# Reordering the token mixers of a two-layer hybrid backbone, with stated queueing

## The chip, the cores and the metric

One core of one Trainium2 chip runs the whole network in one launch. The metric is device time in microseconds (us). The engines are TensorE (PE: matmuls, and PEld: its weight loads), VectorE (DVE), ScalarE (ACT), GpSimd (POOL) and the DMA queue that SyncE (SP) issues. Each engine takes its instructions strictly in the order in which the program lists them.

## The reference, cut to what matters

Two layers; each is a half-step SwiGLU, a token mixer, and another half-step SwiGLU on 256 context and 256 latent tokens of width 1024. The mixer normalises, projects with one wide matrix `w_in`, runs four branches and merges them:

```
p = split(xn @ w_in)                       # ssm z, xbc, dt | mlstm qk, v, o, gates | s5 u | gdn qkv, z, b, a | 4 merge gates
ya = rmsnorm((ssd_scan(conv(xbc), dt) + d * x) * silu(z))          # ssm, chunks of 128, both directions
yb = rmsnorm(mlstm_scan(conv(qk), v, gates)) * sigmoid(o)          # ml
yc = glu(gelu(s5_scan(u)))                                         # s5: complex linear recurrence
yd = rmsnorm(gdn_scan(conv(qkv), beta, decay)) * silu(z)           # gdn: inverts a unit lower triangle per chunk
h += gate * ((sum_k sigmoid(g_k) * (y_k @ w_branch[k])) @ w_out)
```

Layer 0 needs all 512 tokens of the output; layer 1 needs only the 256 latent ones, so there many products have 256 columns instead of 512. All products are float32 in quality: each is three matmuls of values split into a high and a low part.

## The kernel before, in words

A projection (`proj`, L384) makes two output tiles of 128 rows. For it `weights` (L360) loads two blocks of weights by DMA on SP, ScalarE rounds each to its high part (L366), VectorE subtracts to get the low part (L371), and TensorE runs 48 matmuls (L380 to L382). Three buffers of weights run ahead. A projection that feeds a branch with a convolution ends in `conv`: four multiply-adds per tile on VectorE (L788). The normalised input lies in four tiles, the "x" slots (high and low, two each), with the context tokens in columns 0 to 255 and the latent ones in 256 to 511.

The branches are Python generators, and `mix` (L1749) runs them step by step by a string, `MIX_ORDER` (L1706): `ml:3` runs ml on by three yields, `i4` is the gdn projection of tiles 4 and 5, `g2` the eight tiles of merge gate 2, `m2` merges branch 2. The order in the string is a priority only. When the program is complete, a planner places every engine's instructions by a timeline of its own: whatever it believes ready goes first, and the string decides among what is ready. If it believes that an operation ends earlier than it does, an instruction that needs the result is placed early, and what stands behind it on that engine waits with it.

What the change touches:
- `gates` (L600), the step `rows`: per-token decays and gates; its transposes (L714) need an exponential on ScalarE (L711).
- `s5_scan` (L1593): 256 matmul records (L1606), 32 copies out of PSUM on ScalarE (L1614, L1615), then the recurrence, 63 times four operations of 128x64 on GpSimd (L1620 to L1623).
- `s5` (L1626): its first step copies the states on ScalarE (L1640, L1641) and VectorE (L1642 to L1644), then come four 1 MB tables, matmuls with them (L1661), and the gelu.
- `ml` (L965): uses GpSimd for a memset, for a copy and for weighting q (L1043); its matmuls are L1001, L1028, L1049 and L1054.
- `ssm` (L848): loads and transposes (L865), states, then one step per chunk (L904 to L936; matmuls L932), with products on VectorE (L925) and GpSimd (L927).
- `inverse` (L1085) in gdn: 31 steps of two operations on GpSimd (L1115, L1117), a DMA out (L1119) and back (L1125), and then matmuls.
- `merge_branch` (L1723): loads a branch's output into an x slot (L830), splits it into two more (L375, L376), and multiplies. An x slot is free only when the last projection that reads it is done.

Of the kernel before, what the change touches and what calls it, by code (L numbers as in the profile page):

```python
# [22 lines left out]
class Net:  # L23
# [227 lines left out]
    def rsqrt(self, y, src, scale):  # L251
# [108 lines left out]
    def weights(self, W, k0, nk, c0, nw=256):  # L360
# [17 lines left out]
    def mm3(self, out, ah, al, bh, bl, start, stop):  # L378
# [186 lines left out]
class Gates:  # L565
# [34 lines left out]
    def gates(self, l, P):  # L600
# [145 lines left out]
class Ssm:  # L746
# [100 lines left out]

    def ssm(self, l, P, G, o0, dz):  # L848
# [47 lines left out]
        y = self.t8(9, [128, 4, T])  # L896
        for c in range(o0, 4):
# [7 lines left out]
            for d in range(2):  # L905
                eg = self.t8(1 - d, [128, 2, 8, 128])
# [31 lines left out]
        z = self.get(2, dz, t0)  # L938
# [10 lines left out]
class Ml:  # L949
    def ml_in(self, l, P, o0):  # L950
        nc = self.nc
        W = self.A["w_in"][l]
        t0 = o0 * 128
        self.dM = self.scratch("mlqk", [4, 128, T])
        self.dV = self.scratch("mlv", [4, 128, T])
        self.conv_in(W, 1552, (2, 0), [t0, 0, 0, 0], P["ml_cw"], P["ml_cb"], self.dM)

        def done(c, p):
            v = self.kf([128, 256])
            nc.scalar.copy(v, p)  # L960
            nc.sync.dma_start(self.dV[c][:, j * 256:j * 256 + 256], v)
        for j in range(2):
            self.proj_tok(W, 2064 + j * 256, 8, done)

    def ml(self, l, P, G, o0, do):  # L965
# [9 lines left out]
        for c in range(4):  # L975
            nc.gpsimd.memset(va[c][:, :, 128:130], 1.0)
# [12 lines left out]
        for e in range(2):  # L989
            nc.gpsimd.tensor_copy(so[e * 64:e * 64 + 64], sov[e * 64:e * 64 + 64, :, :, :, e])  # L990
# [24 lines left out]
        for c in range(o0, 4):  # L1015
# [15 lines left out]
            for d in range(2):  # L1031
# [38 lines left out]
        self.rsqrt(ss[:, o0:], ss[:, o0:], 1.0 / 128)  # L1070
# [13 lines left out]
class Gdn:  # L1084
    def inverse(self, LT):  # L1085
# [840 lines left out]
```

## Time and profile before

| | us |
|---|---|
| median of 3 runs (2892.4 to 2896.47) | 2895.95 |
| the profiled execution | 2895.82 |
| its span, first to last instruction | 2894.1 |

| engine | busy us | share |
|---|---|---|
| PE | 2727.4 | 94% |
| DVE | 1664.8 | 58% |
| ACT | 1134.2 | 39% |
| POOL | 781.0 | 27% |

The mean granted TensorE clock is 0.965 of full speed. The mixer of layer 0 takes about 480 to 1245 us of the span, that of layer 1 about 2108 to 2695; the SwiGLU parts lie around them. In a table by stretches a row gives the stretch, its length, busy microseconds of each engine with the number of its instructions in brackets, the granted clock (1.00 is 2.4 GHz, 0.50 is 1.2 GHz), the busy share of the DMA engines and GB/s. A row of waits gives the waiting instruction, what released it, the sum, the number of waits, and the longest.

### The profile page before, as it was taken

To read this page: it belongs to the slowest core of one execution; us is meant where nothing else is said; L and a number is where in the kernel's file an instruction comes from. 1 tells how busy PE (TensorE), PEld (TensorE's weight loads), DVE (VectorE), ACT (ScalarE), POOL (GpSimd) and SP (SyncE) were. 2 spreads that over 40 slices of the span, in tenths; PEclk is the share of its full clock that TensorE was granted. 3 is DMA by queue.
4 is the path that set the end of the run, shared out by engine and by line. 5 is a ranking of instruction groups with operands and counts; after the bars stand their busy time and mean duration, and the time that the engine had idled before them with its cause. 6 is when DMAs were issued, how large, how long until landed. Compare 5 with 4: busy or idle time off the path is not lost.

```text
span 2894.1 us, 46233 instructions
## 1 busy us (share of the span) xinstructions
PE 2727.4 (94%) x17710; PEld 2287.2 (79%) x17710; DVE 1664.8 (58%) x3035; ACT 1134.2 (39%) x1743; POOL 781.0 (27%) x1210
## 2 busy tenths in 40 slices
PE   7999999979998999999999999999988789979999
PEld 5777679767776878796768897778977678978999
DVE  6655345456975546574333476554553788756655
ACT  4322224634544533242212353223455456633444
POOL 1442001492002361430000014420107812634100
PEclk9999999998999999999999999999999899989999
DMA  8444878545545554557763353453484467754554
GB/s 264 122 155 138 271 264 225 136 127 175 175 149 157 157 149 138 194 178 260 239 225 95 99 164 120 133 157 96 155 196 131 133 200 212 225 161 149 172 186 146
DMA packets 509820, 494.19 MB, mean 171 GB/s; under 512 B 79380, under 2 KB 437838, under 8 KB 508574
## 3 DMA queue, kind: packets, MB, share of 16 engines
q1 hardware_dynamic: 509598, 491.22, 56.2%
q8 instruction: 140, 2.29, 0.3%
q14 instruction: 82, 0.67, 0.1%
HBM read 429.17 MB, written 61.96 MB: 170 GB/s over the span
## 4 chain that ended last, share of the span: by engine, by line
PE 69%; POOL 12%; DMA 6%; issue 5%; DVE 4%; ACT 3%; SPq 1%; POOLq 0%; DVEq 0%; ACTq 0%
PE ffn.pb L380 15%; PE ffn.pb L381 15%; PE ffn.pb L382 15%; PE ffn.ps L187 2%; POOL s5scan.t L1623 2%; POOL s5scan.s5m L1620 2%; POOL s5scan.s5m L1622 2%; POOL s5scan.s5m L1621 2%; POOL gdn.t L1117 2%; POOL gdn.gpr L1115 2%; DMA ssm.t<-rows.rowd 1%; PE gates.pb L380 1%; PE gates.pb L381 1%; PE gates.pb L382 1%; PE merge.pb L380 1%
## 5 line engine op out<-in xcount | busy, mean ns | idle before, releaser
L371 DVE TENSOR_TENSOR ffn.wl<-ffn.wf,ffn.wh 128x1024 fp32r<-128x1024 f32 (+1 forms) x308 | 370.3, 1202 | 376.2 <-ACT ffn.wh L366 368.6
L366 ACT CAST ffn.wh<-ffn.wf 128x1024 fp32r<-128x1024 f32 (+1 forms) x308 | 310.4, 1008 | 554.1 <-PE ffn.pb L382 398.8
L382 PE MATMUL ffn.pb<-ffn.t,ffn.wh 128*128 128x256 f32 (+1 forms) x1312 | 438.4, 336 | 0.0
L381 PE MATMUL ffn.pb<-ffn.t,ffn.wl 128*128 128x256 f32 (+1 forms) x1312 | 438.1, 336 | 0.0
L380 PE MATMUL ffn.pb<-ffn.t,ffn.wh 128*128 128x256 f32 (+1 forms) x1312 | 434.5, 337 | 1.0 <-ACT ffn.t L344 1.0
L380 PEld LDWEIGHTS ffn.pb<-ffn.t,ffn.wh 128*128 128x128 f32 x1312 | 244.0, 189 | 34.4 <-ACT ffn.wh L366 4.2
L382 PEld LDWEIGHTS ffn.pb<-ffn.t,ffn.wh 128*128 128x128 f32 x1312 | 246.4, 188 | 29.9 <-issue 2.4
L381 PEld LDWEIGHTS ffn.pb<-ffn.t,ffn.wl 128*128 128x128 f32 x1312 | 247.2, 188 | 28.3 <-issue 1.6
L380 PE MATMUL ffn.pb<-wout.t,ffn.wh 128*128 128x256 f32 (+1 forms) x720 | 242.5, 338 | 0.9 <-ACT wout.t L344 0.9
L381 PE MATMUL ffn.pb<-wout.t,ffn.wl 128*128 128x256 f32 (+1 forms) x720 | 241.3, 336 | 0.0
L382 PE MATMUL ffn.pb<-wout.t,ffn.wh 128*128 128x256 f32 (+1 forms) x720 | 238.9, 335 | 0.0
L313 POOL TENSOR_TENSOR norm.kf<-norm.kf,norm.kf 128x256 f32<-128x256 f32 x45 | 41.9, 930 | 517.9 <-ACT norm.kf L311 506.8
L381 PE MATMUL gates.pb<-ffn.t,gates.wl 128*128 128x512 f32 (+1 forms) x512 | 174.6, 342 | 3.4 <-DVE gates.wl L371 3.4
L380 PE MATMUL gates.pb<-ffn.t,gates.wh 128*128 128x512 f32 (+1 forms) x512 | 173.7, 342 | 0.3 <-ACT gates.wh L366 0.3
L382 PE MATMUL gates.pb<-ffn.t,gates.wh 128*128 128x512 f32 (+1 forms) x512 | 173.9, 341 | 0.0
L380 PEld LDWEIGHTS ffn.pb<-wout.t,ffn.wh 128*128 128x128 f32 x720 | 137.4, 191 | 26.5 <-ACT ffn.wh L366 7.5
L381 PEld LDWEIGHTS ffn.pb<-wout.t,ffn.wl 128*128 128x128 f32 x720 | 136.1, 189 | 16.2 <-DVE ffn.kf L497 0.8
L382 PEld LDWEIGHTS ffn.pb<-wout.t,ffn.wh 128*128 128x128 f32 x720 | 135.0, 188 | 16.0 <-issue 0.8
L380 PE MATMUL ffn.pb<-t,ffn.wh 128*128 128x512 f32 x352 | 142.1, 404 | 2.0 <-DVE ffn.kf L492 1.9
L381 PE MATMUL ffn.pb<-t,ffn.wl 128*128 128x512 f32 x352 | 142.4, 405 | 0.0
L382 PE MATMUL ffn.pb<-t,ffn.wh 128*128 128x512 f32 x352 | 139.5, 402 | 0.0
L371 DVE TENSOR_TENSOR gates.wl<-gates.wf,gates.wh 128x1024 fp32r<-128x1024 f32 x64 | 82.8, 1296 | 61.5 <-ACT gates.wh L366 61.1
(573 smaller groups left out, 6332.9 us busy)
## 6 DMA issues: line engine op xcount, KB each, us to landing
ffn.wf<-in_ffn_up_dram SPq DMA_DIRECT2D x176, 512.0 KB
ffn.t<-in_ada_w_dram SPq DMA_DIRECT2D x68, 1024.0 KB
ffn.wf<-in_ffn_down_dram SPq DMA_DIRECT2D x104, 512.0 KB
gates.wf<-in_w_in_dram SPq DMA_DIRECT2D x64, 512.0 KB
merge.wf<-in_w_branch_dram SPq DMA_DIRECT2D x32, 512.0 KB
zs.wf<-in_w_in_dram SPq DMA_DIRECT2D x24, 512.0 KB
gdnin.wf<-in_w_in_dram SPq DMA_DIRECT2D x24, 512.0 KB
wout.wf<-in_w_out_dram SPq DMA_DIRECT2D x24, 512.0 KB
```

Of the source, the lines that this page charges most:

```text
L187: nc.tensor.matmul(pm[32 * k:32 * k + 32, :], lhsT=self.sF[:, h * 4 + k, 28 - 4 * i:60 - 4 * i], rhs=ws[h][:, k], start=(h == 0), stop=(h ...
L366: nc.scalar.copy(wh[:, :nk, :nw], wf[:, :nk, :nw])
L371: self.w_split = nc.vector.tensor_tensor(wl[:, :nk, :nw], wf[:, :nk, :nw], wh[:, :nk, :nw].bitcast(F32), op=OP.subtract)
L380: mm(out, lhsT=ah, rhs=bh, start=start, stop=False)
L381: mm(out, lhsT=al, rhs=bh, start=False, stop=False)
L382: mm(out, lhsT=ah, rhs=bl, start=False, stop=stop)
L1115: pt_(pr, Lo[:, j + 1:, j].unsqueeze(2).to_broadcast([128, n, m]), Z[:, j, :m].unsqueeze(1).to_broadcast([128, n, m]), op=OP.mult)
L1117: pt_(Z[:, j + 1:, :m], Z[:, j + 1:, :m], pr, op=OP.subtract)
L1620: tt(m[:, 0], at(n - 1), P["A8"][:, 0], op=OP.mult)
L1621: tt(m[:, 1], at(n - 1)[:, ::-1], P["A8"][:, 1], op=OP.mult)
L1622: tt(m[:, 0], at(n), m[:, 0], op=OP.add)
L1623: tt(at(n), m[:, 0], m[:, 1], op=OP.add)
```

## The change

1. The order is written in finer units (two tiles: `q0`, `v0`, `c2`, `zS0`, `ga1` to `gd1` for a quarter of a merge gate), and a step can be marked. `'` puts its TensorE instructions behind the last matmul of the projection traced before it; `!` puts also its ScalarE, VectorE and SP instructions behind that projection's rounding, subtraction and weight load. There are 16 marked steps in layer 0 and 12 in layer 1.
2. ssm runs before the s5 outputs: s5's three steps follow ssm's last one, the first marked `!`. ssm writes its output over its input and uses other slots; the s5 tables get four slots instead of two.
3. `rows` and the inverse are cut into more steps, so that their matmuls can be placed later.
4. ml uses no GpSimd: memset, copy, the product L1043 and the small power (L258) go to VectorE.
5. Half of the 32 copies of `s5_scan` (L1615) go from ScalarE to VectorE.
6. The inverse is split by columns: the first 12 on VectorE, the others on GpSimd.
7. In layer 1 the merges use halves of the x tiles: branch output and splits of the first two lie in the context columns, which no projection reads after the convolutions.

```diff
+        self.w_cast = nc.scalar.copy(wh[:, :nk, :nw], wf[:, :nk, :nw])
...
+        self.last_mm = mm(out, lhsT=ah, rhs=bl, start=False, stop=stop)
...
-        self.rsqrt(ss[:, o0:], ss[:, o0:], 1.0 / 128)
+        self.rsqrt(ss[:, o0:], ss[:, o0:], 1.0 / 128, 0)
...
-            pr = self.gp.tile([128, 256], F32, tag="gpr", name=self.nm("gpr"), bufs=2)[:, :n * m].rearrange("p (a b) -> p a b", a=n)
-            pt_(pr, Lo[:, j + 1:, j].unsqueeze(2).to_broadcast([128, n, m]),
+            for op, c0, c1 in ((nc.vector.tensor_tensor, 0, min(j + 1, 12)), (pt_, 12, j + 1)):
+                m = c1 - c0
...
-                    nc.scalar.copy(o(slice(64, 128), slice(31, None, -1)), pv[64:128, :, :, cs])
+                    nc.vector.tensor_copy(o(slice(64, 128), slice(31, None, -1)), pv[64:128, :, :, cs])
...
-            tb = self.t8(1 + b % 2, [128, R, m, 256])
+            tb = self.t8((5, 6, 1, 2)[b], [128, R, m, 256])
...
-    "rows load s5in s5scan oM loc mlin ml:3 s5:1 ml:1 ssmin s5:1 ml:3 zS i4 glu ssm:2 i6 ssm:3 i8 ssm:1 "
-    "i10 gdn:1 i2 i0 ssm:1 gdn:2 g1 gdn:11 g2 g0 zG out g3 m1 m2 m3 m0",
-    "load rows s5in s5scan mlin loc oM ml:4 ssmin s5:1 ml:1 s5:1 ml:2 i4 i6 zS ssm:2 glu ssm:2 gdn:1 "
-    "ssm:3 i8 i10 i0 i2 gdn:12 zG gdn:1 g1 g2 g0 g3 out m2 m1 m3 m0",
+    "rows:1 load s5in oM0 s5scan rows:1 oM2 loc q2 q0 v0 v1 ml:2 c0 'ml:1 c2 'ml:1 c4 'ml:1 c6 'ml:1 zS0 zS2 'ml:1 i4 "
+    "'ssm:1 i6 'ssm:1 i8 'ssm:1 i10 'ssm:1 i2 'ssm:1 i0 'ssm:1 ga1 'ssm:1 !s5:1 gb1 's5:1 gc1 s5:1 gdn:1 gd1 gdn:1 ga2 "
+    "gdn:6 glu gb2 gc2 gd2 ga0 gb0 gc0 gd0 zG0 zG2 ga3 !gdn:1 gb3 'gdn:6 gc3 gd3 out m1 m2 m3 m0",
+    "load rows:1 s5in q2 s5scan q0 'rows:1 v0 loc v1 oM0 oM2 ml:2 c0 'ml:1 c2 'ml:1 c4 c6 ml:1 zS0 'ssm:1 zS2 i4 'ssm:1 "
+    "i6 'ssm:1 i8 'ssm:1 i10 'ssm:1 !s5:1 i0 i2 's5:1 zG0 s5:1 zG2 gdn:1 ga2 gdn:1 gb2 gdn:6 "
+    "gc2 glu gd2 ga1 gb1 gc1 gd1 ga0 gb0 gc0 gd0 !gdn:1 ga3 gb3 'gdn:6 gc3 gd3 out m2 m1 m3 m0",
...
+HALVES = ((0, 1, 2), (3, 0, 1), (2, 4, 5), (3, 6, 7))
...
+            yH, yL = (self.half(i, F32R) for i in HALVES[S["n"]][1:])
...
+    def half(self, i, dt):
+
+        c = i // 4 * 256
+        t = (self.xH + self.xL)[i % 4][:, :, c:c + 256]
...
+            f, behind = f.lstrip("'!"), {"'": 1, "!": 4}.get(f[0], 0)
+            with ExitStack() as st:
+                for h in (self.last_mm, self.w_cast, self.w_split, self.w_dma)[:behind]:
+                    st.enter_context(self.tc.issue_after(h.ins))
+                step(f)
```

## Rows read from the trace of the kernel before

**Rows 1.** Busy time by stretches: layer 0 in three, layer 1 in three.

```profile
480.00:550.00 70.00, 63.98 (x558) 53.57 (x557) 25.75 (x68) 44.33 (x74) 6.79 (x30) 0.91 0.83 174
550.00:850.00 300.00, 274.75 (x1487) 225.25 (x1486) 213.05 (x439) 131.01 (x203) 117.97 (x256) 0.94 0.51 155
850.00:1245.00 395.00, 370.10 (x2295) 306.56 (x2294) 214.42 (x361) 148.65 (x233) 151.20 (x149) 0.96 0.52 156
2108.00:2200.00 92.00, 80.42 (x769) 72.80 (x768) 43.13 (x98) 56.83 (x94) 19.53 (x51) 0.93 0.70 161
2200.00:2440.00 240.00, 196.87 (x1367) 169.14 (x1366) 179.66 (x357) 115.50 (x196) 126.56 (x246) 0.90 0.56 164
2440.00:2695.00 255.00, 224.04 (x2107) 218.82 (x2107) 166.94 (x297) 114.91 (x191) 119.22 (x133) 0.91 0.65 189
```

**Rows 2.** What TensorE waited for, whole span; the longest nine sums within the mixers.

```profile
PE merge.pb L380 <- ACT merge.t L375: 15.1, 1, 15.1
PE ml.ps L1054 <- POOL ml.k L1043: 14.7, 4, 6.2
PE ssm.ps L932 <- DVE ssm.t L925: 13.8, 8, 6.1
PE ml.ps L1049 <- DVE ml.t L1037: 12.2, 1, 12.2
PE ssm.ps L865 <- DMA ssm.t<-ssmin.ssm: 8.5, 3, 6.8
PE ml.ps L1001 <- POOL s5scan.s5m L1622: 8.0, 1, 8.0
PE rows.ps L714 <- ACT rows.k L711: 6.7, 1, 6.7
PE s5scan.ps L1606 <- ACT s5scan.t L1615: 6.6, 6, 2.0
PE s5.ps L1661 <- ACT s5.t L1641: 6.1, 2, 5.0
```

**Rows 3.** What VectorE, ScalarE and the DMA queue waited for on GpSimd.

```profile
DVE s5.t L1642 <- POOL s5scan.t L1623: 15.2, 1, 15.2
...
DVE s5.t L1642 <- POOL s5scan.t L1623: 13.1, 1, 13.1
...
ACT s5.t L1640 <- POOL s5scan.t L1623: 15.3, 1, 15.3
...
SPq L1119 <- POOL gdn.t L1117: 13.3, 1, 13.3
```

**Rows 4.** Groups by line, ScalarE, 526 to 552 us: count, busy us, mean ns.

```profile
L1614 ACT COPY s5scan.t<-s5scan.ps 64x256 f32<-64x256 f32 x16 | 9.6, 600 | 0.3
L1615 ACT COPY s5scan.t<-s5scan.ps 64x256 f32<-64x256 f32 x16 | 9.5, 592 | 0.2
```

**Rows 5.** Three stretches of 10 us, columns as in rows 1.

```profile
590.00:600.00 10.00, 10.00 (x70) 9.16 (x69) 0.00 (x0) 0.29 (x1) 8.82 (x30) 1.00 0.08 29
640.00:650.00 10.00, 6.54 (x33) 5.26 (x31) 7.69 (x15) 4.87 (x9) 9.37 (x17) 1.00 0.25 79
...
2530.00:2540.00 10.00, 10.00 (x91) 10.00 (x90) 7.41 (x8) 5.61 (x8) 9.37 (x9) 1.00 0.84 252
```

**Rows 6.** GpSimd, layer 1: the recurrence's first operation (start, us), and the inverse by lines.

```profile
2184.87 0.33 POOL L1620 TENSOR_TENSOR s5scan.s5m<-s5scan.t,prep.a 128x64 f32<-128x64 f32 x1 [18.30 <-ACT s5scan.t L1615]
...
L1117 POOL TENSOR_TENSOR gdn.t<-gdn.t,gdn.gpr 128x31 f32<-128x31 f32 (+15 forms) x31 | 24.6, 793 | 2.4
...
L1115 POOL TENSOR_TENSOR gdn.gpr<-gdn.t 128x31 f32<-128x31 f32 (+15 forms) x31 | 22.7, 732 | 24.1 <-DMA gdn.t<-gdn.gl 21.8
```

**Rows 7.** Groups by line, VectorE: two products of two tensors, long and short.

```profile
L1008 DVE TENSOR_TENSOR ml.t<-ml.t,ml.mso 128x260 f32<-128x260 f32 x4 | 1.9, 486 | 3.9 <-ACT ml.t L1006 3.9
...
L268 DVE TENSOR_TENSOR gdn.rsq<-gdn.rstd 128x16 f32<-128x16 f32 x3 | 0.5, 174 | 0.1
```

More of the change, by code (lines that the diff above doesn't have):

```diff
@@ L1759, in mix @@
         order = MIX_ORDER[l].split()
-        last = [f for f in order if f == "out" or f[:4] == "ssm:" or f == "ssm"][-1].split(":")[0]
+        last = [f for f in order if f == "out" or "ssm:" in f][-1].lstrip("'!").split(":")[0]
         merged = lambda j: S["merged"][0][:, j] if l else S["merged"][j // 4][:, j % 4]
         self.dG = self.scratch("gdn", [12, 128, T])
+        self.dS = self.scratch("ssm", [8, 128, T])
+        self.dM = self.scratch("mlqk", [4, 128, T])
+        self.dV = self.scratch("mlv", [4, 128, T])
+        S.update({n: self.scratch(n, [4, 128, T]) for n in ("oM", "zS", "zG")})
         self.dGt = {}
-        make = {"ml": lambda: self.ml(l, P, S["G"], o0, S["oM"]), "s5": lambda: self.s5(l, P, S["G"], o0),
-                "ssm": lambda: self.ssm(l, P, S["G"], o0, S["zS"]), "gdn": lambda: self.gdn(l, P, S["G"], o0)}
+        make = {"rows": lambda: self.gates(l, P),
+                "ml": lambda: self.ml(l, P, self.G, o0, S["oM"]), "s5": lambda: self.s5(l, P, self.G, o0),
+                "ssm": lambda: self.ssm(l, P, self.G, o0, S["zS"]), "gdn": lambda: self.gdn(l, P, self.G, o0)}
+        zs = {"oM": (2576, self.sig_in), "zS": (0, self.silu_in), "zG": (5152, self.silu_in)}
         def step(f):
@@ L1805, in step @@
                 y = {0: self.dssm, 1: self.dml, 2: self.ds5, 3: S["y3"]}[k]
+                S["n"] = S.get("n", -1) + 1
                 if k < 3 or last == "ssm":
[L1807 removed]
+                    if l:
+                        src, y = y, self.half(HALVES[S["n"]][0], F32)
+                        for j in range(4):
+                            nc.sync.dma_start(y[:, j], src[j][:, t0:])
+                    else:
+                        y = self.get("x", y, t0)
                 if "merged" not in S:
                     S["merged"] = [self.t8(9, [128, 8, 256])] if l else [self.t8(8), self.t8(9)]
[L1810 removed]
+                self.merge_branch(l, P, k, y, merged, o0, not S["first"], S)
                 S["first"] = True
@@ L1813, in step @@
                 raise ValueError(f)
+        stages = {"load": "s5scan", "glu": "s5", "loc": "s5", "out": "gdn"}
+        kinds = {"g": "gates", "i": "gdnin", "m": "merge", "c": "ssmin", "q": "mlin", "v": "mlin", "o": "zs", "z": "zs"}
         for f in order:
+            f, behind = f.lstrip("'!"), {"'": 1, "!": 4}.get(f[0], 0)
             n = f.split(":")[0]
-            self.stage = {"load": "s5scan", "glu": "s5", "loc": "s5", "out": "gdn", "oM": "zs", "zS": "zs", "zG": "zs"}.get(
-                n, {"g": "gates", "i": "gdnin", "m": "merge"}[f[0]] if f[0] in "gim" and f[1].isdigit() else n)
-            step(f)
+            self.stage = n if n in make or n in ("s5in", "s5scan") else stages.get(n) or kinds[n[0]]
+            with ExitStack() as st:
+                for h in (self.last_mm, self.w_cast, self.w_split, self.w_dma)[:behind]:
+                    st.enter_context(self.tc.issue_after(h.ins))
+                step(f)
         self.stage = "wout"
```

119 lines of the change are left out of this document (60 added, 59 removed).

## The prediction, made before the changed kernel was run

> **What bounds the kernel now.** I read the engines' shares first: TensorE is busy 94% of the span, so a change of order can only win TensorE's idle time and its slow time. Then the busy time by stretches [rows 1]: outside the two mixers TensorE is almost always busy, inside them it is not. In layer 0 the idle time is 70.0 - 63.98 = 6.0, 25.3 and 24.9 us, in layer 1 11.6, 43.1 and 31.0: 142 us in all. After idle time the rows show a granted clock below 1.00. What that costs is at most (1 - clock) times TensorE's busy time: 5.8 + 16.5 + 14.8 + 5.6 + 19.7 + 20.2 = 83 us, less where the slow time fell into idle time. So 142 + 83 = 225 us is the most that this change could ever bring.
>
> Then the waits of TensorE [rows 2]. The nine listed make 15.1 + 14.7 + 13.8 + 12.2 + 8.5 + 8.0 + 6.7 + 6.6 + 6.1 = 91.7 us of the 142; the remaining 50 us are many small ones. Three of the nine name GpSimd or its recurrence only indirectly, so I asked who waits for GpSimd [rows 3]. VectorE stood 15.2 us in layer 0 and 13.1 in layer 1 at the state copies of s5 (L1642), ScalarE 15.3 us at L1640, and SP 13.3 us at the DMA out of the inverse (L1119). That is the pattern of the whole kernel: an instruction that needs GpSimd's result stands too early in an in-order queue, and what TensorE needs (ml's products at L1037, weight splits, the load for the first merge) stands behind it. The planner thinks GpSimd faster than it is.
>
> **The change, part by part.**
>
> 1. *s5's first step goes behind ssm, and ml leaves GpSimd.* With L1640 and L1642 behind ssm's last step, the recurrence should have ended when they come. ml's product L1043 no longer queues behind it. From rows 2 go 14.7 (L1054), 12.2 (L1049) and 8.0 (L1001): 34.9 us, all of it. VectorE gets these small operations, a few us in each layer; in the same rows its load is 180 of 240 us at the highest [rows 1], and I price this under 7. The reciprocal root of 8 elements in layer 1 becomes twelve VectorE operations of about 0.17 us [rows 7], 2 us beside projections: nothing.
>
> 2. *`rows` cut in two.* In layer 1 the transposes L714 stood in TensorE's queue ahead of mlin's matmuls and waited 6.7 us for an exponential. Now they are stated behind `q0`. All 6.7 go.
>
> 3. *Half of the copies to VectorE.* 16 x 0.600 + 16 x 0.592 = 19.1 us of ScalarE [rows 4] become 9.6, beside 16 copies on VectorE, which has 25.75 us of work in the 70 us of layer 0's first stretch and 43.13 of 92 in layer 1's [rows 1]. The 6.6 us at L1606 shrink with ScalarE's part, which is still as long as the matmuls between: I take 5. Nothing would go if a strided copy on VectorE took 1.2 us, twice ScalarE's 0.600; all 6.6 if it took less than that 0.600.
>
> 4. *ssm ahead of the s5 outputs.* The 6.1 us at L1661 (ScalarE's copies after the recurrence) go. But at the new place the copies, then two of the four table loads, have only one projection as cover, and two of the tables need slots that ssm gives back last. The trace shows no such place. From below it costs nothing (the copies move under `gb1`); from above what L1661 waits now, 6.1, in each layer. I take 4 per layer, 8.
>
> 5. *Marked ssm steps.* TensorE waits 13.8 us at L932 in 8 waits and 8.5 us at L865 (loads that wait for a slot or for the convolution's DMA). With a whole projection queued ahead of each chunk, VectorE and GpSimd get that projection's time to make the operands. In layer 1 the load has only `zS0`, 256 columns. I take half of 22.3, so 11. Full gain is the other end; the other is zero, if VectorE is late anyway.
>
> 6. *Inverse by columns, and merges in halves.* In layer 1 the inverse's POOL operations take 24.6 + 22.7 = 47.3 us [rows 6]. Step j has (31 - j)(j + 1) products, 5456 in all; columns from 12 on are 1330 of them in 19 steps. So GpSimd keeps 38 of 62 operations and 24% of the elements: between 0.24 x 47.3 = 11.4 us and 38/62 x 47.3 = 29. VectorE gets 62 operations with 4126/31 = 133 elements on average. Nearest rows: 0.174 us for 16 elements, 0.486 for 260 [rows 7]; linearly 0.32 us, 62 x 0.32 = 20 us (10.8 to 30). Even with GpSimd and VectorE in turn this is no longer than now. Before, TensorE had run out of projections; now `gc2` to `gd0` stand between, ten units and glu, eleven times 48 matmuls at 91 per 10 us [rows 5], 58 us. SP's 13.3 us at L1119 end while weights are still there, and the first two merges of layer 1 no longer need the x slots that the last gate reads. The 15.1 us at L380 go, all. If that cover were gone (inverse in turn and 20 us late) 15 would come back.
>
> 7. *What is paid.* VectorE: from 2200 to 2440 us it has 179.7 us of work [rows 1]. Its own work hardly moves out of there, and ml's products come in. If this stretch gave back its share of everything it would shrink to some 200 us, VectorE at 90%. Convolutions and ssm or ml chunks now alternate strictly, so I take back 20 us over both layers. Each of the 28 marked steps can also make TensorE stand at a chunk that VectorE has not finished. Seven are ml's; today's mean wait at an ssm chunk, 13.8 / 8 = 1.7 us [rows 2], gives 7 x 1.7 = 12. The gdn scan at the end keeps its small waits but may lose some merge matmuls as filler: 8, an estimate, about the sum of two waits of 4.
>
> Sum of idle time: 34.9 + 6.7 + 5 + 6.1 + 11 + 15.1 = 78.8, and a third of the unlisted 50, 17: 96 us, 68% of 142. Clock: 68% of 83 is 56; a slow stretch partly lies in the idle time already counted, so three quarters, 42. Gross 138. Back: 8 (under 4) + 20 + 12 + 8 = 48. Net 90. Against the profiled execution's own 2895.82 us this is 2805.8; the median of the runs, 2895.95, is the same within 0.13. I forecast 2806 us.
>
> A rule that speaks against the change: GpSimd and VectorE do not simply work side by side. With VectorE idle the recurrence makes 30 operations in 10 us, with VectorE busy 7.69 of 10 only 17 [rows 5]. The Trainium skill ("SBUF — State Buffer", section on the two separate sides) says why: VectorE with two SBUF inputs and GpSimd reading SBUF exclude each other for a whole instruction. The rows agree with a loss of that kind. By the rule the split inverse takes the sum of its parts, 31 us or more, not the longer part, 20; both are under the cover. What it could change is the recurrence, the second rival.
>
> **The rivals.**
>
> *All gaps close.* VectorE keeps up and the marked steps cost nothing: 96 + 56 and a little more of the small waits, 150 us, 2746. For it: in 850 to 1245 us and at the end VectorE is at 54% and 65% only [rows 1]. Against: 2200 to 2440.
>
> *VectorE becomes the bound and holds GpSimd back.* The copies that made VectorE stand 13 to 15 us [rows 3] are gone, so it works more while the recurrence runs. It has 4 x 63 = 252 operations. At 17 per 10 us all of it takes 148 us, at 30 it takes 84. In layer 1 it starts at 2184.87 now [rows 6], after 2 and 3 (6.7, and half of 19.1) about 16 us earlier, 2169, and ends at 2253 to 2317. ssm's first chunk wants its products L927 behind it on GpSimd. Between lie `q0` to `i6`: seven units of full width and six of half, 7 x 10.6 + 6 x 5.3 = 106 us, and ml's and ssm's own matmuls; so from 2275 on. Late by up to 40 us, 1 is not won but moved to ssm: 12.2 us and half of 14.7, 19.6, stay in layer 1, 5's 11 too, and 15 of the clock; 46 less than forecast: 2852.
>
> *Slower.* The place: TensorE's queue at the 28 marked steps. Projections behind a marked step wait for it, as they need not now, and a mark is worth nothing where VectorE comes later than the projection ahead ends. Without any wait at marked steps the change wins 138 - 8 - 20 - 8 = 102 us. Each us of mean wait costs 28, and slow clock in today's proportion (1 + 83/142 = 1.58), 44 us. So it decides at 102 / 44 = 2.3 us for each step. At the 3.7 us that L1054 waits on average now (14.7 / 4, rows 2) it costs 163: 61 us slower, 2957. For it: L932's longest wait, 6.1. Against: its mean, 1.7 [rows 2], and my 11 + 12 us over the 19 steps of ml and ssm is 1.2.
>
> *It doesn't do what it says.* The planner keeps its wrong idea of GpSimd and finds another early place for the marked steps' successors; or the halves of x are held as whole tiles. Then the idle time only changes its place: 2896.
>
> **How the numbers follow.** The forecast (2770 to 2838) has 0.53, all gaps close (2700 to 2770) 0.13, VectorE bound (2838 to 2872) 0.20, smaller gains (2872 to 2890) 0.02, no change 0.04, slower 0.08. Three runs of this kernel span 0.14%, so about 0.2% (5.8 us) is what a measurement tells from no change. Faster is 0.53 + 0.13 + 0.20 + 0.02 = 0.88. The range reaches from the middle of the first rival past the end of the second, 2730 to 2880.
>
> **What would show it.** Right: no wait of VectorE or ScalarE on the recurrence above 3 us; no wait of ml's matmuls on GpSimd; the first merge of layer 1 begins while gates still run; the clock in both mixers at 0.95 or more; ScalarE with 16 copies in s5_scan. Wrong: waits of TensorE on VectorE at L932, L1049 or the new place of L1661 with sums above 30 us; ssm waiting for GpSimd; VectorE above 90% between layer 1's second convolution and its gates with TensorE below 80%. The prediction fails as a whole if the mixers' idle time stays above 110 us.

## The result, and the profile after

The changed kernel takes 2850.91 us (median of 4 runs, 2845.56 to 2852.84) against 2894.76 of the kernel before beside it: ratio 0.985, 95% interval 0.983 to 0.986. That is 44 us faster, half of the 90 that were forecast. The time lies in the range, but outside the forecast's own range of 2770 to 2838. The profiled execution takes 2849.91 us, its span 2848.2.

The busy time by stretches, the same six as in [rows 1], with ends moved to where these parts now lie (columns as there):

```profile
477.00:549.00 72.00, 66.18 (x589) 55.85 (x590) 36.48 (x94) 32.83 (x57) 14.32 (x47) 1.00 0.74 166
549.00:800.00 251.00, 234.39 (x1250) 192.73 (x1249) 190.91 (x397) 110.97 (x182) 109.47 (x217) 0.97 0.52 156
800.00:1217.00 417.00, 397.69 (x2506) 329.83 (x2505) 259.21 (x478) 169.63 (x258) 129.31 (x129) 0.95 0.54 167
2079.00:2160.00 81.00, 71.52 (x708) 64.58 (x707) 49.43 (x116) 37.56 (x64) 15.97 (x46) 0.94 0.68 161
2160.00:2390.00 230.00, 205.13 (x1459) 179.58 (x1458) 189.19 (x376) 122.61 (x204) 125.08 (x236) 0.95 0.62 188
2390.00:2649.00 259.00, 221.66 (x2078) 217.08 (x2078) 179.01 (x363) 115.80 (x197) 96.94 (x109) 0.90 0.60 179
```

TensorE's idle time (length minus PE) is now 5.8 + 16.6 + 19.3 in layer 0 and 9.5 + 24.9 + 37.3 in layer 1: 113 us, 29 less than the 142 before. The clock's cost, worked out as in the prediction, falls from 83 to 7 + 20 + 4 + 10 + 22 = 63 us. Together this is 49, about the 44. The last stretch of layer 1 got worse: 37.3 us idle, 31.0 before.

The waits of TensorE within the mixers, nine longest sums and two small ones, against [rows 2]:

```profile
PE gdn.ps L1150 <- DMA gdn.k<-gdn.gz: 16.8, 1, 16.8
PE ssm.ps L930 <- DVE ssm.t L923: 8.9, 9, 1.8
PE s5scan.ps L1606 <- DMA s5scan.t<-prep.s5K: 8.1, 1, 8.1
PE ml.ps L1042 <- issue: 7.3, 2, 6.9
PE zs.pb L380 <- ACT zs.wh L366: 6.3, 2, 5.3
PE zs.pb L381 <- DVE zs.wl L371: 5.8, 4, 2.9
PE gates.pb L381 <- DVE gates.wl L371: 5.7, 2, 4.0
PE mlin.pb L380 <- ACT mlin.wh L366: 5.2, 1, 5.2
PE merge.pb L380 <- DVE merge.t L1754: 4.6, 3, 2.7
...
PE s5scan.ps L1606 <- DMA s5scan.t<-s5in.s5U: 2.4, 1, 2.4
...
PE ssm.ps L863 <- DMA ssm.t<-ffn.ssm: 2.0, 2, 1.4
```

("issue" is time in which the engine waited for nothing that the profile shows.) ml's waits on GpSimd are gone, so are those of `rows` and of s5's outputs. The wait for the inverse (L1150, the products behind the DMA out of it and back) has grown from 4.7 us to 16.8. New are the loads of the s5 scan (L1606) and most of the waits for weights that are rounded (L366) or split (L371): 6.3 + 5.8 + 5.7 + 5.2 + 1.3 = 24.3 us, 7.1 before. No wait of VectorE or ScalarE on the recurrence [rows 3] is left.

The inverse in layer 1, its products and its subtractions (start of the first and of the last, and median time of one), against [rows 6]:

```profile
L1114 DVE TENSOR_TENSOR gdn.gpr<-gdn.t x31: 170/335/561, 2478.1 to 2530.2; 128x60 f32<-128x60 f32 x2, 128x156 f32<-128x156 f32 x2, 128x192 f32<-128x192 f32 x2, 128x31 f32<-128x31 f32 x1
L1114 POOL TENSOR_TENSOR gdn.gpr<-gdn.t x19: 221/370/1320, 2478.2 to 2501.9; 128x19 f32<-128x19 f32 x2, 128x36 f32<-128x36 f32 x2, 128x51 f32<-128x51 f32 x2, 128x64 f32<-128x64 f32 x2
...
L1116 DVE TENSOR_TENSOR gdn.t<-gdn.t,gdn.gpr x31: 170/340/822, 2479.4 to 2530.4; 128x60 f32<-128x60 f32 x2, 128x156 f32<-128x156 f32 x2, 128x192 f32<-128x192 f32 x2, 128x31 f32<-128x31 f32 x1
```

VectorE's 62 operations take 21.0 us in sum but stand over 52 us, because other work of VectorE's lies between them in its queue, 15 weight subtractions of 19.7 us above all. GpSimd's part ends at 2502. TensorE has no projection left at 2518.6 and stands until 2535.4. Its clock falls during this stand; stretches of the changed kernel around it, and three of VectorE's busiest:

```profile
2200.00:2250.00 50.00, 47.06 (x295) 40.23 (x292) 45.42 (x102) 23.94 (x36) 46.63 (x86) 0.97 0.46 127
2250.00:2300.00 50.00, 45.86 (x231) 37.02 (x229) 48.25 (x96) 23.70 (x42) 29.00 (x44) 1.00 0.64 197
2300.00:2350.00 50.00, 45.96 (x369) 41.77 (x367) 46.59 (x89) 28.06 (x50) 3.90 (x3) 0.97 0.61 189
...
2478.00:2531.00 53.00, 36.12 (x303) 35.01 (x301) 49.34 (x107) 18.23 (x24) 30.91 (x46) 0.92 0.79 248
...
2519.00:2523.00 4.00, 0.00 (x0) 0.00 (x0) 4.00 (x8) 0.84 (x1) 3.08 (x4) 0.96 0.51 164
2523.00:2557.00 34.00, 19.24 (x378) 18.91 (x380) 15.63 (x44) 7.27 (x12) 6.30 (x6) 0.50 0.28 75
```

VectorE is busy 45.4, 48.3 and 46.6 of 50 us, and 49.3 of the 53 us of the inverse. From 2523 to 2557 us the granted clock is 0.50, the lower level; the first 12 us of this belong to the stand.

### The profile page after: what moved, and what is told of

Its sections match the earlier page's. It is cut to its first block, busy times and chain, and to the rows that moved or that the text cites. A ratio compares the mean times of both kernels' runs of the same rounds, so it can differ in the third digit from the quotient of the medians.

```text
span 2848.2 us, 46282 instructions
## 1 busy us (share of the span) xinstructions
PE 2710.5 (95%) x17710; PEld 2278.2 (80%) x17710; DVE 1724.6 (61%) x3234; ACT 1110.8 (39%) x1711; POOL 730.6 (26%) x1129
## 4 chain that ended last, share of the span: by engine, by line
PE 79%; DVE 6%; DMA 6%; issue 3%; ACT 2%; POOL 2%; SPq 1%; DVEq 0%; POOLq 0%; ACTq 0%
PE ffn.pb L380 15%; PE ffn.pb L381 15%; PE ffn.pb L382 15%; PE gates.pb L381 2%; PE gates.pb L380 2%; PE gates.pb L382 2%; PE ffn.ps L187 2%; DMA ssm.t<-rows.rowd 2%; PE merge.pb L380 1%; PE merge.pb L381 1%; PE merge.pb L382 1%; PE gdnin.pb L382 1%; PE gdnin.pb L381 1%; PE gdnin.pb L380 1%; PE mlin.pb L452 1%
## 5 line engine op out<-in xcount | busy, mean ns | idle before, releaser
L371 DVE TENSOR_TENSOR ffn.wl<-ffn.wf,ffn.wh 128x1024 fp32r<-128x1024 f32 (+1 forms) x308 | 370.3, 1202 | 377.4 <-ACT ffn.wh L366 367.5
L366 ACT CAST ffn.wh<-ffn.wf 128x1024 fp32r<-128x1024 f32 (+1 forms) x308 | 310.4, 1008 | 556.0 <-PE ffn.pb L382 398.6
L381 PE MATMUL ffn.pb<-ffn.t,ffn.wl 128*128 128x256 f32 (+1 forms) x1312 | 438.3, 336 | 0.0
L380 PE MATMUL ffn.pb<-ffn.t,ffn.wh 128*128 128x256 f32 (+1 forms) x1312 | 434.7, 338 | 1.0 <-ACT ffn.t L344 1.0
L380 PEld LDWEIGHTS ffn.pb<-ffn.t,ffn.wh 128*128 128x128 f32 x1312 | 244.1, 189 | 34.2 <-ACT ffn.wh L366 4.2
L381 PEld LDWEIGHTS ffn.pb<-ffn.t,ffn.wl 128*128 128x128 f32 x1312 | 247.3, 189 | 28.3 <-issue 1.6
L380 PE MATMUL ffn.pb<-wout.t,ffn.wh 128*128 128x256 f32 (+1 forms) x720 | 242.5, 338 | 0.9 <-ACT wout.t L344 0.9
L381 PE MATMUL ffn.pb<-wout.t,ffn.wl 128*128 128x256 f32 (+1 forms) x720 | 241.4, 336 | 0.0
L381 PE MATMUL gates.pb<-ffn.t,gates.wl 128*128 128x512 f32 (+1 forms) x512 | 178.8, 350 | 5.7 <-DVE gates.wl L371 5.7
L380 PE MATMUL gates.pb<-ffn.t,gates.wh 128*128 128x512 f32 (+1 forms) x512 | 177.1, 348 | 1.9 <-ACT zs.kf L807 1.8
L382 PE MATMUL gates.pb<-ffn.t,gates.wh 128*128 128x512 f32 (+1 forms) x512 | 176.5, 346 | 0.0
L380 PEld LDWEIGHTS ffn.pb<-wout.t,ffn.wh 128*128 128x128 f32 x720 | 137.5, 191 | 26.5 <-ACT ffn.wh L366 7.5
L381 PEld LDWEIGHTS ffn.pb<-wout.t,ffn.wl 128*128 128x128 f32 x720 | 136.1, 189 | 16.2 <-issue 0.8
L380 PE MATMUL ffn.pb<-t,ffn.wh 128*128 128x512 f32 x352 | 142.2, 404 | 2.1 <-DVE ffn.kf L493 1.9
L381 PE MATMUL ffn.pb<-t,ffn.wl 128*128 128x512 f32 x352 | 142.1, 404 | 0.0
L381 PEld LDWEIGHTS gates.pb<-ffn.t,gates.wl 128*128 128x128 f32 x512 | 99.8, 195 | 17.9 <-DVE gates.wl L371 6.3
```

The lines of the kernel that those rows point to most:

```text
L366: self.w_cast = nc.scalar.copy(wh[:, :nk, :nw], wf[:, :nk, :nw])
L371: self.w_split = nc.vector.tensor_tensor(wl[:, :nk, :nw], wf[:, :nk, :nw], wh[:, :nk, :nw].bitcast(F32), op=OP.subtract)
L380: mm(out, lhsT=ah, rhs=bh, start=start, stop=False)
L381: mm(out, lhsT=al, rhs=bh, start=False, stop=False)
L382: self.last_mm = mm(out, lhsT=ah, rhs=bl, start=False, stop=stop)
```

## The experiments

Two theories after the first look. T1: layer 1 ends on gdn's chain, which starts late and whose inverse is stretched. T2: VectorE's load holds TensorE in layer 1 wherever the order puts the work. A ratio is to the kernel before on the same chip; differences to the changed kernel (ratio 0.9846) are in units of 2895 us, and uncertain by some 7 to 10 us.

I also use the length of each mixer in the profiled executions, from the first matmul of `s5in` to the last of the merges. Where layer 0 is the same code as in the changed kernel (746.6) it came out at 746.3, 749.2, 749.8 and 756.0, so differences under 10 us say nothing.

```
                                   layer 0   layer 1 (us)
before                               773.8     563.6
changed                              746.6     546.0
changed, inverse's steps left out    753.4     527.0
changed, inverse on GpSimd alone     753.8     544.5
changed, layer 1 without L371        749.8     509.0
changed, the same, gdn earlier*      756.0     519.0
before, layer 1 without L371         776.4     507.8
changed, ml on GpSimd                755.3     548.7
changed, s5 ahead of ssm             775.9     564.8
changed, three edits                 739.2     546.4
```

(* Layer 1 without L371, and gdn's chain earlier in it.)

**The inverse left out.**

```diff
-        for j in range(31):
+        for j in range(0):
```

> The 31 steps of the inverse are left out in both layers (its input and output transfers stay; the inverse is then the identity). Theory T1: layer 1 of the changed kernel ends on gdn's chain. The chain starts 22 us later after the mixer's start than before, its inverse takes 52 us (2478 to 2530) although VectorE works only 21 us on it, and TensorE then stands 16.8 us and runs at half clock for 34 us. By T1 about 16.8 + half of 20 to 34 goes: 25 to 32 us faster than the changed kernel, 2819 to 2826 us. Theory T2: VectorE's load holds TensorE everywhere and the chain hides beside it; then only 2 x 21 us of VectorE's work goes, most of it beside other work: under 8 us, 2843 or more.

2830.18 us, ratio 0.979 (0.978 to 0.981): 16 us faster than the changed kernel, between the two. Layer 1 becomes 19 us shorter, less than the inverse's 52, and layer 0 no shorter.

**The column split undone.**

```diff
-            for op, c0, c1 in ((nc.vector.tensor_tensor, 0, min(j + 1, 12)), (pt_, 12, j + 1)):
+            for op, c0, c1 in ((pt_, 0, j + 1),):
```

> Only the column split of the inverse is undone, all of it on GpSimd. T1: 47 us of GpSimd work in layer 1 against 52 us from first to last operation now, so the chain is as long as before and the time the same: 2845 to 2857 us. T2: VectorE is relieved of 42 us over both layers: 10 to 20 us faster, 2831 to 2841. The reason given before the run of the change (shorter inverse, 20 instead of 47 us) would make this 15 to 30 us slower.

2855.51 us, ratio 0.988 (0.986 to 0.991): 11 us slower, the direction of the third expectation and less than its size. The mixers don't show where: layer 0 is 7.2 us longer, but so it is, by 6.8, with the inverse's steps left out. In layer 1 the inverse on GpSimd alone ran from 2481 to 2536, 55 us, against 52 split: beside VectorE's weight subtractions the split wins next to nothing.

**The halves of x undone.**

```diff
-        if l:
+        if False:
```

> Only the halves of x are undone: layer 1's merges take whole x tiles again, so none starts before the last gate. T1: TensorE had run out of work before the inverse ended anyway, and the two early merges fill part of that; without them 0 to 8 us slower, 2850 to 2859. The forecast's reason: the old wait of 15.1 us is back on top, 2862 to 2872.

2842.22 us, ratio 0.984 (0.982 to 0.985): no difference. The old wait comes back (L380 on ScalarE's L375), but with 3.9 us instead of 15.1. The halves are worth nothing here.

**gdn's chain earlier in layer 1.**

```diff
-i0 i2 's5:1 zG0 s5:1 zG2 gdn:1 ga2 gdn:1 gb2 gdn:6 gc2 glu
+i0 gdn:1 's5:1 i2 gdn:1 s5:1 glu gdn:6 zG0 zG2 ga2 gb2 gc2
```

> Changed kernel with another order in layer 1: the gdn loads come between the s5 steps, glu directly behind them, and the third to eighth gdn step ahead of zG0 zG2 ga2 gb2 gc2, five projections of 5.3 us. T1: gdn's chain starts up to 27 us earlier, 15 to 25 us faster than the changed kernel: 2826 to 2836. T2: no change, within 5 us of 2851.

2841.62 us, ratio 0.984 (0.982 to 0.987): no difference. The inverse does start 38 us earlier (2440.3), and the wait of 16.8 us is gone, but this run's waits of TensorE from 2300 to 2400 us are new:

```profile
PE ssm.ps L930 <- DVE ssm.t L923: 11.6, 2, 7.7
PE gdn.ps L1205 <- DMA gdn.k<-ffn.gdn: 6.4, 2, 5.2
PE ssm.ps L283 <- ACT ssm.k L839: 5.6, 2, 5.1
```

In the changed kernel L930 waits 1.4 us there. What the order took from one place came back in another. That speaks for T2, though not by a full VectorE alone: it is busy 46.4 us of the 50 from 2300, but 22.1 of the 40 from 2350, where TensorE is idle 15.9. So I took VectorE's load away.

**No weight subtraction in layer 1's mixer.**

```diff
+        if getattr(self, "light", False):
+            self.w_split = self.w_cast
+            return wh, wh
         self.w_split = nc.vector.tensor_tensor(wl[...], wf[...], wh[...], op=OP.subtract)
```

> In layer 1's mixer all of VectorE's weight subtractions (L371) are left out, 95 of about 1.25 us in the trace of the changed kernel, some 118 us of its work; the matmuls read the high part in their place, so TensorE's work is the same and the products are wrong by a factor. Theory A, VectorE is the limit of layer 1 (busy 91 to 97% from 2200 to 2350 us and 94% from 2480 to 2530): the inverse takes about 21 us instead of 52, the gap of 16.8 us and the slow stretch of 34.1 behind it go, and the small waits for split weights too: 30 to 40 us faster than the changed kernel, 2811 to 2821. Theory B, the latency of gdn's own chain (DMAs, small transposes and waits in turn) sets the end of layer 1: the gap of 16.8 us stays above 10, and the time is 2838 to 2850.

2811.52 us, ratio 0.974 (0.971 to 0.977): 31 us faster, as theory A said. The inverse (here L1120) is not stretched any more, and TensorE waits 1.4 us at it:

```profile
L1120 DVE TENSOR_TENSOR gdn.t<-gdn.t,gdn.gpr x31: 172/322/453, 2446.8 to 2469.9; 128x60 f32<-128x60 f32 x2, 128x156 f32<-128x156 f32 x2, 128x192 f32<-128x192 f32 x2, 128x31 f32<-128x31 f32 x1
```

Its busy time in layer 1's last two stretches; 15.5 and 8.3 us idle:

```profile
2160.00:2390.00 230.00, 214.48 (x1558) 191.30 (x1551) 146.78 (x353) 129.16 (x218) 104.45 (x239) 0.94 0.66 200
2390.00:2586.00 196.00, 187.74 (x1820) 185.24 (x1819) 103.40 (x284) 94.96 (x162) 69.21 (x101) 0.92 0.66 200
```

**The same, and gdn's chain earlier.** Both edits above.

> The same work left out as in the run beside it, and the order of layer 1 in which gdn's chain starts earlier, which alone changed the time by under 2 us (it opened 26 us of waits in 2330 to 2382 us, at ssm's chunks and the norms). Theory A (VectorE full): these waits go with VectorE's load, so TensorE has no idle stretch of over 5 us between 2250 and 2530: 2800 to 2815, at or below the run beside it. Theory B (latency of the chains of ssm and gdn): the waits at ssm's chunks stay at 15 us or more, and the time is that of the run beside it or above, by up to 15 us.

2816.53 us, ratio 0.975 (0.972 to 0.978): 4 us behind the run beside it, inside the uncertainty, and a miss for theory A by number. ssm's waits (L930's line) did shrink from 16.8 us with gdn earlier alone to 6.2, but gdn's transposes (L1205's) waited 10.0 us for the DMA of gdn's inputs. Earlier is no better in either case; that an earlier gdn is limited by its own loads is likely, not shown.

**The marks left out.**

```diff
-            f, behind = f.lstrip("'!"), {"'": 1, "!": 4}.get(f[0], 0)
+            f, behind = f.lstrip("'!"), 0
```

> The marks are left out of the order (nothing is stated to stand behind a projection), the order is the same. By the prediction's own terms the marks give 11 us at ssm and cost 12: within 6 us of the changed kernel, 2845 to 2857. Rival, the marks are what keeps the planner's early placing from returning: waits of TensorE on GpSimd or VectorE of 6 to 15 us at ml, ssm or s5 come back, 15 to 35 us slower, 2866 to 2886. Second rival, the marked steps hold TensorE: 10 us or more faster, below 2841.

2846.62 us, ratio 0.986 (0.983 to 0.988): no difference. In the two traces, compared group by group of a tile's instructions, the work of TensorE, GpSimd and the DMA queue stands in the same order throughout both mixers, that of VectorE and ScalarE in all but a place or two. So the marks placed nothing here that the order's text had not placed already.

**s5's outputs ahead of ssm again.** The order alone, in both layers; here layer 1:

```diff
-c6 ml:1 zS0 'ssm:1 zS2 i4 'ssm:1 i6 'ssm:1 i8 'ssm:1 i10 'ssm:1 !s5:1 i0 i2 's5:1 zG0 s5:1 zG2 gdn:1
+c6 ml:1 zS0 !s5:1 zS2 's5:1 i4 s5:1 i6 'ssm:1 i8 'ssm:1 i10 'ssm:1 i0 'ssm:1 i2 zG0 zG2 gdn:1
```

The slots stay those of the changed kernel, so ssm's chunk buffers now share two slots with s5's outputs. The values change in this run; the amount of work does not.

> The s5 outputs go back ahead of ssm in both layers, with the marks kept at the same places of the order and all else as in the changed kernel. Theory of the prediction (what ScalarE and VectorE lost waiting for the recurrence at the state copies was the largest term): VectorE and ScalarE stand 10 to 15 us again at the copies in each layer, and TensorE at what is queued behind: 20 to 35 us slower than the changed kernel, 2871 to 2886. Rival (ml off GpSimd and the finer order did it, the place of s5 is nothing): 2845 to 2857.

2893.5 us, ratio 1.001 (0.999 to 1.003): the whole gain is gone, more than expected. The waits that the theory named are there: ScalarE and VectorE on the recurrence at the state copies, in layer 0 (12.2 us, and 10.4 for VectorE) and in layer 1.

```profile
ACT s5.t L1641 <- POOL s5scan.t L1623: 12.2, 1, 12.2
...
ACT s5.t L1641 <- POOL s5scan.t L1623: 19.0, 1, 19.0
DVE s5.t L1643 <- POOL s5scan.t L1623: 16.0, 1, 16.0
```

Weights that ScalarE rounds come late behind them (L366 at `zs` and `gdnin`). But the larger sum of TensorE's waits in this run stands elsewhere:

```profile
PE gdn.ps L1150 <- DMA gdn.k<-gdn.gz: 68.1, 2, 37.4
PE zs.pb L380 <- ACT zs.wh L366: 22.7, 2, 20.7
...
PE gdnin.pb L380 <- ACT gdnin.wh L366: 7.5, 1, 7.5
```

With ssm later, gdn's chain is later too (layer 0's inverse begins at 1067.5 us, in the changed kernel at 997.9), and TensorE runs out of projections before it. But ssm is late by the shared slots. The loads of its chunk buffers (L742) wait for the gated unit's matmuls and its store:

```profile
SPq L742 <- DMA s5.ys<-s5.t: 4.0, 1, 4.0
SPq L742 <- PE s5.pb L382: 0.5, 1, 0.5
```

The first of them starts at 847.0 us in layer 0 and at 2411.5 in layer 1, when these matmuls end; in the changed kernel at 549.0 and 2162.6. So the run prices the place of s5 together with the slots given to it, which part 4 did not do: both set when gdn begins. How much the place is worth alone stays open.

**The subtractions left out of the kernel before.** The same edit in the kernel before.

> The kernel before, with the same work left out as in the run where it was left out of the changed kernel (VectorE's weight subtractions L371 in layer 1's mixer, some 118 us of VectorE; the products are wrong by a factor). There it made the kernel 1.1% faster (ratio 0.974 against 0.985), 31 us. Theory A', the change made VectorE the limit of layer 1, as the prediction's part 7 says: before, its load (74 to 82% in 2230 to 2380 us) cost little, so this run is 5 to 14 us faster than the kernel before, ratio 0.995 to 0.998, and 17 to 26 us is what the limit took of the change. Rival, VectorE's load cost the kernel before as much: ratio 0.988 to 0.991, and the limit explains nothing of what is missing.

2835.65 us, ratio 0.981 (0.980 to 0.983): 54 us faster, beyond the rival. So theory A' falls. The change did not make VectorE's load the limit of layer 1; this load cost the kernel before already, and more: 54 us before, 31 after. The busy time of this run from 2200 us on, against [rows 1]; TensorE is idle 23.3 us from 2200 to 2440, and 43.1 in [rows 1]:

```profile
2200.00:2440.00 240.00, 216.73 (x1587) 190.10 (x1587) 149.31 (x352) 139.10 (x246) 122.70 (x248) 0.96 0.64 197
2440.00:2610.00 170.00, 165.49 (x1677) 163.59 (x1675) 76.22 (x193) 77.25 (x120) 71.06 (x106) 0.95 0.67 202
```

With that load gone layer 1 takes 507.8 us in the old order and 509.0 in the new one: there the change is worth nothing but its better dealing with a loaded VectorE.

The edit takes away more than room in VectorE's queue, and the paths are not separated. TensorE's waits for split weights can't be much of it: they were 3.4 us of the mixer's waits in layer 1 (L381 at `gates`). GpSimd can: beside less work of VectorE's it is faster. The recurrence, 128 us long in the kernel before, takes 113 here, and the unsplit inverse 37 instead of 52, with the same operations (L1120 here is L1117 in [rows 6], 793 ns on average there):

```profile
L1120 POOL TENSOR_TENSOR gdn.t<-gdn.t,gdn.gpr 128x31 f32<-128x31 f32 (+15 forms) x31 | 16.9, 546 | 2.4
```

**ml back on GpSimd.**

```diff
-                        tt(qw[q], qk[q, 0:2, sl], rw[q, 8 + d * 4 + e:8 + d * 4 + 4:2], op=OP.mult)
+                        nc.gpsimd.tensor_tensor(qw[q], qk[q, 0:2, sl], rw[q, 8 + d * 4 + e:8 + d * 4 + 4:2], op=OP.mult)
...
-        self.rsqrt(ss[:, o0:], ss[:, o0:], 1.0 / 128, 0)
+        self.rsqrt(ss[:, o0:], ss[:, o0:], 1.0 / 128)
```

> In the changed kernel ml's memset, its copy, its weighting of q and the root of its 8 sums go back to GpSimd, behind or among the recurrence; the order stays. By the prediction's part 1 the waits of ml's matmuls on GpSimd come back (34.9 us in the kernel before) with some slow clock: 25 to 45 us slower than the changed kernel, 2876 to 2896. Rival, ml is on time now even on GpSimd, since its steps stand elsewhere, or the waits turn into nothing behind other work: within 8 us, 2843 to 2859.

2865.11 us, ratio 0.991 (0.989 to 0.993): 19 us slower than the changed kernel, less than the theory's 25 and nearer to it than to the rival. The wait at ml's products comes back:

```profile
PE ml.ps L1047 <- POOL ml.k L1036: 21.1, 3, 9.2
```

**The s5 scan one projection later.**

```diff
-oM0 s5scan rows:1 oM2 ... q2 s5scan q0 'rows:1
+oM0 oM2 s5scan rows:1 ... q2 q0 s5scan 'rows:1
```

> Only the order: one projection more stands ahead of the s5 scan's matmuls in each layer (oM2 in layer 0, q0 in layer 1), which waited 2.4 and 8.1 us for their loads in the trace of the changed kernel, with 10.2 us of slow clock behind the second. The recurrence then starts some 10 us later; its states are used over 60 us after its end. If these waits are a price of the change by itself (the prediction's 8 under part 4): 8 to 14 us faster, 2837 to 2843. If the time is set behind them, by ml's operands and VectorE: the gap moves to ml or ssm, within 5 us, 2846 to 2856.

2839.1 us, ratio 0.983 (0.981 to 0.985): 4 us faster, inside the uncertainty. The wait for the loads went from 8.1 to 5.5 us in layer 1, and in layer 0 none over 1.5 us is left of the 2.4. (These loads are not what part 4 set its 8 us for; that is the tables of s5's outputs.)

**Three edits, for a better kernel.**

```diff
-gd3 out m2 m1 m3 m0
+gd3 out m2 m1 m0 m3
...
-        nc.vector.tensor_scalar(h, h, 0.5, 0.5, op0=OP.mult, op1=OP.add)
+        if not raw:
+            nc.vector.tensor_scalar(h, h, 0.5, 0.5, op0=OP.mult, op1=OP.add)
...
+                nc.vector.scalar_tensor_tensor(mg if first else g, g, 1.0, p, op0=OP.add, op1=OP.mult)
...
+        nc.vector.tensor_scalar(gate, gate, 0.5, None, op0=OP.mult)
```

> Three edits of the changed kernel together. (1) One projection more ahead of the s5 scan's matmuls, as in the run before (4 us faster there). (2) The merge gates store tanh, and the merge multiplies by (tanh + 1) with half of it taken into the output gate: VectorE loses 32 operations of 0.38 us in layer 1, 12 us, and as many longer ones in layer 0. (3) In layer 1 the merge of ssm's branch (96 matmuls, 11.9 us) stands ahead of gdn's products instead of last, where TensorE stood 16.8 us. If TensorE's idle time before gdn's products is only missing work: the 16.8 us shrink to under 6, most of the slow stretch of 34.1 us with them, two merges after gdn become one, and the whole is 18 to 30 us faster than the changed kernel, 2821 to 2833. If VectorE's load sets when the inverse ends: the merge brings it some 12 us of subtractions, splits and products, as many as edit 2 takes away, so the inverse ends no earlier and up to 8 us later, half of the merge is won: 8 to 17 us faster, 2834 to 2843. If both only move the wait: within 6 us of the run before.

2832.05 us, ratio 0.979 (0.976 to 0.982): faster than both kernels, 17 us below the changed one by the ratios, uncertain by 10. By number that is at the edge of the first expectation; by trace it is not the first. The wait at the inverse and the inverse itself (L1117, 1 line lower than above):

```profile
PE gdn.ps L1151 <- DMA gdn.k<-gdn.gz: 15.2, 1, 15.2
...
L1117 DVE TENSOR_TENSOR gdn.t<-gdn.t,gdn.gpr x31: 170/389/830, 2470.1 to 2532.3; 128x60 f32<-128x60 f32 x2, 128x156 f32<-128x156 f32 x2, 128x192 f32<-128x192 f32 x2, 128x31 f32<-128x31 f32 x1
```

The merge fills TensorE up to 2525.8, and the inverse now takes 62 us instead of 52, with the merge's work on VectorE in it (VectorE is busy 58.6 of the 64 us from 2469). That is the second expectation's mechanism, and layer 1 is as long as before the edits (546.4). Layer 0 is 7 us shorter, inside the spread; where the 17 us lie is open.

## Why the prediction was half right

*What bounds.* That an order can win TensorE's idle and slow time was right; that two thirds of it, 96 of 142 us idle, are there for this order to win was not. In layer 1 the argument read VectorE's 180 of 240 us [rows 1] as an average with room. In pieces, the same trace of the kernel before:

```profile
2230.00:2280.00 50.00, 32.63 (x160) 26.81 (x158) 36.99 (x80) 20.91 (x28) 46.48 (x92) 0.83 0.40 108
2280.00:2330.00 50.00, 39.30 (x260) 31.50 (x261) 35.08 (x76) 20.45 (x31) 31.79 (x67) 0.83 0.57 179
2330.00:2380.00 50.00, 41.17 (x305) 36.23 (x305) 40.95 (x83) 27.18 (x53) 5.27 (x4) 0.90 0.56 170
2380.00:2420.00 40.00, 34.64 (x269) 29.94 (x264) 38.51 (x67) 24.63 (x42) 15.12 (x11) 0.96 0.56 140
```

From 2330 us VectorE has little room or none. But in the two pieces in which TensorE is idle most, 17.4 and 10.7 us, VectorE is busy 37.0 and 35.1 of 50 and stands 13.1 us at L1642, as the argument said. So no share of VectorE's shows the limit there; only the run without the subtractions does.

*Part 1* was right in mechanism: all three waits left, and ml off GpSimd is worth 19 us by the run that undoes it. Priced with 34.9 us of idle time it left 7.3 at L1042 and 3.6 us at ml's loads in their place, so some 24 net.

*Part 2*: the 6.7 us went, but at the same place in layer 1 the s5 scan's matmuls, which now come earlier, wait 8.1 us for their loads (2.4 in layer 0). The sum has nothing for this; by these waits part 2 won nothing. *Part 3*: the wait on ScalarE went; 1.0 us on VectorE's copies is left. *Part 4*: the 6.1 us went, and the 8 us set for the tables at the new place were not paid: no matmul with a table (L1662) waits longer than 0.2 us. These were the small terms; what s5's place and slots do to ssm and gdn was the large one, as the run with s5 ahead shows.

*Part 5*: L932's and L865's 22.3 us became 8.9 + 2.0, a gain of 11.4 against 11 forecast. But the marks do not bring it: without them the order of the queues and the time are the same.

*Part 6 failed.* VectorE's 62 operations take 21.0 us (20 forecast) and GpSimd's 38 take 21.3 (11 to 29), but the inverse lasts 52 us, no less than the 52 of before, since VectorE stands full of splits. The cover of eleven units was used up at 2518.6. The wait of 15.1 us went, but it was not won: L1150 waits 16.8 in its place, L380 4.6 on the merges' products, and the stretch at the lower clock is 34 us long.

*Part 7 was the step that was mis-sized, and for a wrong reason.* 20 us were set for a VectorE that the change fills. The runs show a load of VectorE's that cost as much before: its weight subtractions in layer 1 cost the kernel before 54 us and cost the changed one 31. The forecast counted two thirds of the idle time behind this load as won by the order.

*The small waits.* What no term of the sum names, 50 us before, of which a third was to go, is 113 - 16.8 - 8.9 - 8.1 - 2.4 - 2.0 - 4.6 = 70 us now. In it the waits for rounded or split weights grew from 7.1 to 24.3. Of these 12.8 are splits. The other 11.5 are not the subtractions', and stay without them (8.2 + 4.5): ScalarE stood 5.1 and 4.7 us at a step of ssm's chunk (L910) that needs a load, ahead of the rounding that TensorE needed. Here in layer 1:

```profile
2169.18 1.28 ACT L910 ACTIVATE ssm.t<-ssm.t,rows.gc 128x128 f32<-128x128 f32 x4 [4.71 <-DMA ssm.t<-rows.rowd]
...
2173.95 1.03 ACT L366 CAST zs.wh<-zs.wf 128x1024 fp32r<-128x1024 f32 x1
```

That is the pattern which the change was to remove, with a load in the place of GpSimd.

*The clock* gave back 20 us, not 42: idle time was cut into smaller pieces and its largest piece made anew.

*The rivals.* "VectorE becomes the bound and holds GpSimd back" gave 2852, one us from the result, by luck: another mechanism acted. Nothing waits for the recurrence, so its place was wrong; that VectorE's load bounds was right, but it did so before the change too, and so was GpSimd held back: in layer 1 the recurrence lasts from 2146.4 to 2274.0 us, 128, and 103 in the run without subtractions. "Slower": the marked steps wait 0.99 us on average at L930, far under its 2.3, and the marks it priced moved nothing.

*The signs.* Right: no wait on the recurrence, no wait of ml on GpSimd, 16 copies on ScalarE. Wrong: the first merge begins at 2490.5, when the last gate ends; the clock is 0.90 in the last stretch. And the idle time is 113 us: by its own sign, 110, the prediction's account of the mixers failed. That the time is in the range, 2730 to 2880, is owed to the rivals that it was widened for, not to the sum.

*What earned the 44 us:* layer 0 gave 27.2 and layer 1 17.6. By the runs that undo one part: the place of s5 with its slots (47, all), ml off GpSimd (19), the inverse's split (11). They do not add up, since each also decides what the others are worth.

Left open: an inverse whose operations stand together in VectorE's queue was not tried, nor s5 ahead of ssm with slots of its own, nor weight subtractions on another engine.

## What to carry to other kernels

Before crediting idle time to a new order, cut the stretch into pieces of 50 us and ask whether any engine is full in them; an average over 240 us hides it. Then leave work of the busiest engine out of the kernel before, as an experiment, also where the pieces are not full: it prices that load, on all its paths, before anything is reordered. An experiment that moves a step back must give it back its own buffers too, or it measures both. And a chain of many short operations on a nearly full in-order engine takes the time of everything that the planner puts between them, not its own sum.

## What was not expected of the hardware

VectorE's operations hardly slow down beside other work, GpSimd's do. The inverse's own subtractions take on average, in the changed kernel and then without the weight subtractions (L1120 there):

```profile
L1116 DVE TENSOR_TENSOR gdn.t<-gdn.t,gdn.gpr 128x60 f32<-128x60 f32 (+27 forms) x31 | 10.6, 341 | 0.7
L1116 POOL TENSOR_TENSOR gdn.t<-gdn.t,gdn.gpr 128x19 f32<-128x19 f32 (+9 forms) x19 | 12.0, 631 | 1.5
...
L1120 DVE TENSOR_TENSOR gdn.t<-gdn.t,gdn.gpr 128x60 f32<-128x60 f32 (+27 forms) x31 | 9.9, 319 | 0.9
L1120 POOL TENSOR_TENSOR gdn.t<-gdn.t,gdn.gpr 128x19 f32<-128x19 f32 (+9 forms) x19 | 7.2, 378 | 1.5
```

VectorE goes from 341 to 319 ns, GpSimd from 631 to 378; the recurrence on GpSimd takes 128 us and 103. This agrees with the rule that the prediction took from the Trainium skill ("SBUF — State Buffer", the two separate sides), in that the load of VectorE costs GpSimd time. Its reading there, that the two parts of the inverse would take their sum, does not hold as a price, 31 us or more: without the subtractions both engines together are done in 24 us, in which VectorE is busy 21.7 and GpSimd 13.8.

```profile
2446.00:2470.00 24.00, 22.95 (x202) 22.76 (x202) 21.68 (x72) 13.87 (x19) 13.79 (x38) 1.00 0.90 287
```

That row is of the changed kernel without the subtractions, columns as in [rows 1]; busy time may hold waiting of one engine for the other, so how far they exclude each other stays open. VectorE is busy 90% of that row, and 93% of the 53 us of the inverse in the changed kernel, so its share alone does not set what GpSimd loses; what differs is the weight subtractions of 1.2 us and more among its operations. And a stand of 16.8 us cost more than itself: in the 34 us at the lower clock, of which the first 12 belong to the stand, TensorE did 19.2 us of busy time at half speed, some 10 us more.
